# A transformer trunk layer on one core: the mix-out as seven block products, and five held steps in the down projection

## The chip, the core and the metric

The kernel runs on one core of a Trainium2 chip. The metric is device time in microseconds for one launch, the median of several runs. The core has a matrix engine (PE), two engines for elementwise work (VectorE, DVE in the profile, and ScalarE, ACT), GpSimd (POOL) and SyncE (SP). In this kernel SP and POOL issue nearly all transfers between the chip's memory (HBM) and the on-chip tiles. PE writes its sums into eight PSUM banks of 128 x 512 float32.

## What is computed

One layer with 512 tokens of width 1024, all in float32. Cut to the steps that matter here:

```python
def trunk_layer(x, mem):
    h = rms_norm(x, g[0])
    # four branches of width 256, each projected to 1024 and gated
    branch = jnp.einsum('bskc,kcd->bskd', y_stack, w_branch)
    gates = jax.nn.sigmoid((h @ w_gate).reshape(b, s, 4, 1024) + b_gate)
    merged = jnp.sum(gates * branch, axis=2)
    y = merged @ w_mix_out                        # mix-out, 1024 x 1024
    x = x + rms_norm(y, g[1])
    h = rms_norm(x, g[2]); mem_n = rms_norm(mem, g[4])
    y = cross_attention(h, mem_n, wq, wkv, wo)
    x = x + rms_norm(y, g[3])
    h = rms_norm(x, g[5])
    up = causal_dwconv(h @ w_up, conv_w, conv_b)
    gg, val = jnp.split(up, 2, axis=-1)
    y = (jax.nn.gelu(gg) * val) @ w_down          # down projection, 2816 x 1024
    return x + rms_norm(y, g[6])
```

## The kernel before

**Matmuls.** Every large product is made of float32 operands split in two (`split`, L153; for weights `load_unit`, L69): a rounded high part in the format that PE takes, copied by ScalarE (L75), and the rest, subtracted by VectorE (L76). `mm3` (L127) then issues three matmuls, high by high, high by low, low by high.

**Weights.** All weights are read in units of 128 x 1024 (512 KB) in the order of the list `plan` (L81 to L97). `unit()` hands out the next one and keeps `LOOK` = 2 more under way. A unit passes a raw tile (4 buffers) and a split pair (4 buffers each of `whi`, `wlo`). `unit_kept` (L109) splits into general tiles instead, which stay until they are given back.

**Tiles.** Other data lies in 70 general slots of 128 x 512 (`get` and `put`, L54 to L63), handed out first in, first out when the program is written. A slot's new content waits for the last reader of its old one. PSUM has tags A (2 banks), B (4) and C (2).

**Order.** The build fixes the order on each engine. It goes by the order of the code and by when the build reckons that an instruction can start, so an instruction can stand ahead of earlier code that is not yet ready.

**Stages around the change.**
- *Gates* (L657 to L689): for each of the four branches and each of eight column tiles m, a gate product in bank A (24 matmuls) and a branch product in bank C (6), a sigmoid, a product and a sum into `acc[m]`. In the last branch `acc[m]` is split into `merged`.
- *Memory norm* (L692 to L705): four memory tiles, four rows for the statistics (`RowNorm`), the factor spread over a bank C (`bctok`, four small matmuls), eight products on VectorE and four splits.
- *Mix-out* (L747 to L768): x tiles and gains are loaded, then for each column half four token tiles with K = 1024 in eight tiles, four units per half; each bank is squared for the norm and multiplied by the gain.
- *k projection* (L795 to L808): eight units, 24 matmuls of 256 columns each, two banks A. Its time also holds the end of the mix-out's norm, the residual (L771) and the first transposes for the next stage (`turn2`, tile h2T).
- *Down projection* (L1043 to L1161): two halves of tokens, two parities of K tiles and two halves of columns make 2 x 2 blocks. Instead of eight block products it makes seven: p1, p2, p6, p5 in a first pass over the 11 steps of K, and p3, p7, p4 in a second pass, from sums of the operand blocks (`pair_up`, `second_a`, `second_b`) and of the weight blocks. In each pass the last two steps are held back and run product by product, so that a product's sums on VectorE start while PE makes the next one. `down_post` and `finish` do norm, residual and the stores.
- *Weight sums for the down projection* (L637 to L654): `sums_load(i)` reads four quarters of 256 KB on POOL's queue, `sums(i)` makes four VectorE additions and writes four quarters to `wsum` in HBM. Nine of the eleven stand in the gates, one in three gate units; two stand in the k projection.

Of the kernel before, what the change touches and what calls it, by code (L numbers as in the profile page):

```python
# [16 lines left out]
P = 128  # L17
# [9 lines left out]
LOOK = 2  # L27

# [10 lines left out]
def tile_trunk(ctx: ExitStack, tc: tile.TileContext, a: dict, out: bass.AP):  # L39
# [46 lines left out]
    for nm in ("w_mix", "w_k", "w_v", "w_q"):  # L86
        plan += [(a[nm][m], 1024) for m in range(KT)]
# [8 lines left out]
    for i in range(NP):  # L96
        plan += [(a["w_down"][NP + i][:, S:2 * S], S), (wsum[NP + i], 1024)]  # L97
# [536 lines left out]

    quarters = {}

    def sums_load(i):  # L637
        q = [[get("wq") for _ in R2] for _ in R2]
        for r in R2:
            for c in R2:  # L640
                gpsimd.dma_start(q[r][c], a["w_down"][c * NP + i][:, r * S:(r + 1) * S])
        quarters[i] = q

    def sums(i):
        (b11, b12), (b21, b22) = quarters.pop(i)
# [4 lines left out]
        gpsimd.dma_start(wsum[i][:, 0:S], b11)  # L650
        gpsimd.dma_start(wsum[i][:, S:2 * S], b22)
        gpsimd.dma_start(wsum[NP + i][:, 0:S], b21)
        gpsimd.dma_start(wsum[NP + i][:, S:2 * S], b12)
        put(b11, b12, b21, b22)  # L654


    acc = [None] * KT  # L657
    merged = []
    for ki, kb in enumerate(order):
        for m in range(KT):  # L660
# [46 lines left out]
    LO, HI = slice(0, 256), slice(256, S)  # L707
# [45 lines left out]
    yt = [[None, None] for _ in T4]  # L753
    for c in range(2):
        ps = [bank("B" if c == 0 else "AACC"[t], "mo") for t in T4]
        for kp in range(4):
            tok_unit(ps, merged, T4, kp, unit())
        for t in T4:
            n1.square(ps[t], t, c)
            yt[t][c] = get("yt")  # L760
            vector.tensor_tensor(yt[t][c], ps[t], g1[c], op=ALU.mult)
            if t == 0:
                scalar.activation(warm, n1.ss[:, c * 4:c * 4 + 1], AF.Sqrt, scale=0.0, bias=epsc)
    for t in merged:
        put(*t)
# [238 lines left out]
    def pair_up(i):  # L1004
        g0, g1 = g[2 * i], g[2 * i + 1]
        hi, lo = get("gh", F32R), get("gl", F32R)
        for j, t in enumerate((g0, g1)):
            c = slice(j * 256, (j + 1) * 256)
            scalar.copy(hi[:, c], t[:, LO])
            vector.tensor_tensor(lo[:, c], t[:, LO], hi[:, c].bitcast(F32), op=ALU.subtract)  # L1010
        vector.tensor_sub(g1[:, LO], g0[:, LO], g1[:, LO])
        vector.tensor_sub(g0[:, LO], g0[:, LO], g0[:, HI])
        vector.tensor_sub(g0[:, HI], g1[:, HI], g0[:, HI])
        vector.tensor_add(g1[:, LO], g1[:, LO], g0[:, HI])
        gp1[i] = (hi, lo)
# [30 lines left out]
    def down_post(t, c):  # L1046
        n5.square(yt[t][c], t, c)
        if c == (1 if t < 2 else 0):
            n5.add(t, t + 1)
        vector.tensor_tensor(yt[t][c], yt[t][c], g6[c], op=ALU.mult)  # L1050

    def finish(t):
        n5.root(t, t + 1)
        for c in range(2):
            vector.scalar_tensor_tensor(yt[t][c], yt[t][c], n5.col(t), xt[t][c], op0=ALU.mult, op1=ALU.add)
            sync.dma_start(out[t][:, HALF[c]], yt[t][c])
        put(*yt[t])


# [181 lines left out]
```

## Time and profile before

| What | Value |
|---|---|
| Median of 3 runs | 942.09 us (941.8 to 942.45) |
| Profiled execution | 941.86 us, its span 940.0 us |
| Mean granted PE clock | 0.995 of full speed |
| HBM read, written | 119.25 MB, 13.63 MB |
| Matmuls and transposes on PE | 4534 |
| Weight sums in the trace | 11, from 117.7 to 399.3 us |

Times in the profile count from the start of the span. A row of a group gives line, engine, operation, output and inputs, shape and count, then its busy time and the mean of one, then the engine's idle time before it and what ended it. A row of a timeline gives start, length, engine and the same, with the idle time before it in brackets. `PE` is matmuls and `PEld` weight loads beside them. The chain that ended last is the path followed back from the last instruction.

### The profile page before, as it was taken

What the parts mean: (1) busy time and instruction counts of PE and PEld (TensorE: products, weight loads), DVE (VectorE), ACT (ScalarE), POOL (GpSimd) and SP (SyncE); (2) the same over time, 40 slices, a digit from 0 to 9 for tenths busy, and PEclk for the clock granted to TensorE, in tenths of its full rate; (3) what the DMA queues carried; (4) which work ended last, traced back from release to release, by engine and by line L of the source; (5) the groups of instructions that cost most, each with busy time, mean ns of one, the idle gap of its engine ahead of it and who ended that gap; (6) DMA issues with size and microseconds to landing.
All of it is one profiled execution on the core that took longest, in us unless ns stands there. A gap on an engine that the chain in (4) does not pass through costs nothing.

```text
span 940.0 us, 12070 instructions
## 1 busy us (share of the span) xinstructions
PE 922.4 (98%) x4534; PEld 776.9 (83%) x4534; DVE 606.7 (65%) x940; ACT 441.1 (47%) x707; POOL 56.0 (6%) x117
## 2 busy tenths in 40 slices
PE   8999999999999999999999999999999999999994
PEld 7888888888888888889888888988888888888883
DVE  5877569645665566757544845486666666697847
ACT  7836336422342233456433737453443443465642
POOL 1100022401110000300000000000000000000000
PEclk9999999999999999999999999999999999999997
DMA  9432255835564524745522330133322322355552
GB/s 333 141 130 101 101 190 178 290 133 181 192 227 136 195 94 155 241 140 179 180 90 77 125 112 1 48 110 95 107 90 98 104 90 93 120 178 181 166 191 90
DMA packets 43563, 133.67 MB, mean 142 GB/s; under 512 B 6240, under 2 KB 7152, under 8 KB 43504
## 3 DMA queue, kind: packets, MB, share of 16 engines
q1 hardware_dynamic: 36288, 109.81, 35.5%
q0 software_dynamic: 7072, 23.09, 7.1%
q8 instruction: 35, 0.57, 0.2%
q14 instruction: 24, 0.20, 0.1%
q10 hardware_dynamic: 144, 0.00, 0.0%
HBM read 119.25 MB, written 13.63 MB: 141 GB/s over the span
## 4 chain that ended last, share of the span: by engine, by line
PE 94%; DVE 3%; ACT 2%; DMA 0%; issue 0%; SPq 0%; DVEq 0%; ACTq 0%
PE up L130 8%; PE up L128 8%; PE up L129 8%; PE gate L128 6%; PE gate L129 6%; PE gate L130 6%; PE win L128 4%; PE win L129 3%; PE win L130 3%; PE dn L129 3%; PE dn L128 3%; PE dn L130 3%; PE br L128 2%; PE mo L128 2%; PE q L128 2%; PE q L130 2%
## 5 line engine op out<-in xcount | busy, mean ns | idle before, releaser
L76 DVE TENSOR_TENSOR wlo<-raw,whi 128x1024 fp32r<-128x1024 f32 (+1 forms) x181 | 214.3, 1189 | 155.5 <-ACT whi L75 155.0
L75 ACT CAST whi<-raw 128x1024 fp32r<-128x1024 f32 (+1 forms) x181 | 185.1, 1026 | 276.0 <-issue 78.9
L128 PE MATMUL up<-h3h,whi 128*128 128x512 f32 (+1 forms) x368 | 138.2, 375 | 0.0
L129 PE MATMUL up<-h3l,whi 128*128 128x512 f32 (+1 forms) x368 | 138.1, 375 | 0.0
L130 PE MATMUL up<-h3h,wlo 128*128 128x512 f32 (+1 forms) x368 | 138.1, 375 | 0.0
L128 PE MATMUL gate<-xgh,whi 128*128 128x512 f32 x256 | 99.9, 390 | 0.0
L130 PE MATMUL gate<-xgh,wlo 128*128 128x512 f32 x256 | 99.7, 389 | 0.0
L129 PE MATMUL gate<-xgl,whi 128*128 128x512 f32 x256 | 99.6, 389 | 0.0
L129 PEld LDWEIGHTS up<-h3l,whi 128*128 128x128 f32 x368 | 69.3, 188 | 12.6
L128 PEld LDWEIGHTS up<-h3h,whi 128*128 128x128 f32 x368 | 69.3, 188 | 12.5
L130 PEld LDWEIGHTS up<-h3h,wlo 128*128 128x128 f32 x368 | 69.3, 188 | 12.3
L550 DVE SCALAR_TENSOR_TENSOR c<-up,par,c 128x511 f32<-128x511 f32 (+1 forms) x88 | 65.1, 745 | 1.3
L128 PE MATMUL win<-xgh,whi 128*128 128x512 f32 x144 | 57.2, 397 | 0.0
L128 PEld LDWEIGHTS gate<-xgh,whi 128*128 128x128 f32 x256 | 48.1, 188 | 10.0
L130 PEld LDWEIGHTS gate<-xgh,wlo 128*128 128x128 f32 x256 | 48.1, 188 | 10.0
L130 PE MATMUL win<-xgh,wlo 128*128 128x512 f32 x144 | 56.3, 391 | 0.0
L129 PEld LDWEIGHTS gate<-xgl,whi 128*128 128x128 f32 x256 | 48.1, 188 | 9.8
L129 PE MATMUL win<-xgl,whi 128*128 128x512 f32 x144 | 56.1, 390 | 0.0
L356 DVE TENSOR_TENSOR sg<-gate,rb0s 128x512 f32<-128x512 f32 x32 | 22.0, 688 | 44.5 <-PE gate L130 44.3
L128 PE MATMUL dn<-whi,sh 128*128 128x512 f32 x110 | 42.8, 389 | 0.0
L129 PE MATMUL dn<-wlo,sh 128*128 128x512 f32 x110 | 42.8, 389 | 0.0
L130 PE MATMUL dn<-whi,sl 128*128 128x512 f32 x110 | 42.8, 389 | 0.0
(376 smaller groups left out, 1736.3 us busy)
## 6 DMA issues: line engine op xcount, KB each, us to landing
raw<-in_w_up SPq DMA_DIRECT2D x44, 512.0 KB, 3.4
raw<-in_w_gate SPq DMA_DIRECT2D x32, 512.0 KB, 4.1
wq<-in_w_down POOLq DMA_DIRECT2D x44, 256.0 KB, 3.9
wsum<-wq POOLq DMA_DIRECT2D x44, 256.0 KB, 3.3
raw<-wsum SPq DMA_DIRECT2D x22, 512.0 KB, 3.6
raw<-in_w_in SPq DMA_DIRECT2D x18, 512.0 KB, 3.9
raw<-in_w_down SPq DMA_DIRECT2D x11, 512.0 KB, 4.3
raw<-in_w_br SPq DMA_DIRECT2D x8, 512.0 KB, 3.5
```

Source lines behind the costliest of these rows:

```text
L75: scalar.copy(hi[:, :n], raw[:, :n])
L76: vector.tensor_tensor(lo[:, :n], raw[:, :n], hi[:, :n].bitcast(F32), op=ALU.subtract)
L128: tensor.matmul(ps, lhsT=w[0], rhs=x[0], start=first, stop=False)
L129: tensor.matmul(ps, lhsT=w[0], rhs=x[1], start=False, stop=False)
L130: tensor.matmul(ps, lhsT=w[1], rhs=x[0], start=False, stop=last)
L356: vector.tensor_tensor(t, ps, rb0s, op=ALU.mult)
L550: vector.scalar_tensor_tensor(dst[:, s:S], src[:, 0:S - s], pc(wname, (taps - 1 - s) * stride + off), dst[:, s:S], op0=ALU.mult, op1=ALU.add)
```

## The change

The mix-out is computed as the down projection was: token halves, K parities and column halves form 2 x 2 blocks, four steps of two K tiles, seven products in two passes. The bodies of the down projection move into functions that both stages call: `pair_first`, `pair_a`, `pair_b` make the operand sums, `seven` runs the two passes. In `seven` the last `ha` steps of the first pass and the last `hb` of the second are held: the mix-out has 2 and 2, the down projection 2 and 5 (`HOLD`; it was 2 and 2).

The weight sums of the mix-out (four, into `msum`) go first in the queue of weight sums. The queue is now worked by `sums_step`, in every second gate unit from the sixth, with one set loaded further ahead, and in the k projection's units. The operand sums of the mix-out are made pair by pair in the last branch's gates.

For the last five steps of the down projection's second pass the weights are no longer in `plan` but split with `unit_kept` into general slots, made one step ahead.

```diff
+HOLD = 5
@@ plan
-    for nm in ("w_mix", "w_k", "w_v", "w_q"):
+    msum = dp.tile([8, P, 1024], F32, name="msum")
+    for i in range(4):
+        plan += [(a["w_mix"][i], 1024), (msum[i], 1024)]
+    for i in range(4):
+        plan += [(a["w_mix"][4 + i][:, S:2 * S], S), (msum[4 + i], 1024)]
+    for nm in ("w_k", "w_v", "w_q"):
...
-    for i in range(NP):
+    for i in range(NP - HOLD):
         plan += [(a["w_down"][NP + i][:, S:2 * S], S), (wsum[NP + i], 1024)]
@@ operand sums, moved
+    def pair_b(g0, g1):
+        ah, al, b = get("sh", F32R), get("sl", F32R), get("sb", F32R)
+        scalar.copy(ah, g1)
+        vector.tensor_sub(al, g1, ah.bitcast(F32))
+        scalar.copy(b[:, LO], g0[:, LO])
+        vector.tensor_sub(b[:, HI], g0[:, LO], b[:, LO].bitcast(F32))
+        put(g0, g1)
+        return ah, al, b
@@ the two passes
+    def seven(n, first, opa, opb, wua, wub, ha, hb, ready):
+        bks = [[bank(tag, "sv") for _ in T2] for tag in "BBCA"]
+        held, free_later = [], []
+        for i in range(n):
+            wa, ws = wua(i)
+            a, e = first[i], opa(i)
+            f, l = i == 0, i == n - 1
+            todo = [(bks[0], a, 0, wa(0, S), f, l), (bks[1], a, 256, wa(S, 2 * S), f, l),
+                    (bks[2], e, 256, ws(S, 2 * S), f, l), (bks[3], e, 0, ws(0, S), f, l)]
+            if i < n - ha:
+                for p in todo:
+                    product(*p)
+                put(*a, *e)
+            else:
+                held.append(todo)
+                free_later += [*a, *e]
...
+                elif k == 2:
+                    vector.tensor_sub(d0[t], bks[2][t], yt[t][0])
+                    vector.tensor_add(yt[t][0], yt[t][0], bks[1][t])
+                    ready(t, 0, False)
+                elif k == 3:
+                    vector.tensor_sub(d1[t], d0[t], bks[3][t])
...
+        for k in range(3):
+            for t in T2:
+                for todo in held:
+                    product(*todo[k], ts=(t,))
+                if k == 0:
+                    yt[t][1] = get("yt")
+                    vector.tensor_sub(yt[t][1], d1[t], bks[0][t])
+                    ready(t, 1, True)
+                elif k == 1:
+                    yt[t + 2][1] = d1[t]
+                    vector.tensor_sub(d1[t], d1[t], bks[1][t])
+                    vector.scalar_tensor_tensor(d0[t], d0[t], -1.0, bks[1][t], op0=ALU.mult, op1=ALU.add)
+                    ready(t + 2, 1, False)
+                else:
+                    yt[t + 2][0] = d0[t]
+                    vector.tensor_add(d0[t], d0[t], bks[2][t])
+                    ready(t + 2, 0, True)
@@ weight sums
+    sumq = [(a["w_mix"], i, 4, msum) for i in range(4)] + [(a["w_down"], i, NP, wsum) for i in range(NP)]
+    summing = []
+
+    def sums_step(load=True):
+        if len(summing) > 1 or (summing and not sumq):
+            sums(summing.pop(0))
+        if load and sumq:
+            summing.append(sumq.pop(0))
+            sums_load(summing[-1])
@@ gates
-            step = ki * KT + m - 5
-            if step >= 0 and step % 3 == 0:
-                sums_load(step // 3)
-            if step >= 2 and step % 3 == 2:
-                sums(step // 3)
+            if ki * KT + m >= 5 and (ki * KT + m - 5) % 2 == 0:
+                sums_step()
...
-                if ki == 3:
-                    merged.append(split(acc[m], "mg", True))
+                if ki == 3 and m % 2 == 1:
+                    pair = acc[m - 1], acc[m]
+                    mix_first.append(pair_first(*pair))
+                    mix_a.append(pair_a(*pair))
+                    mix_b.append(pair_b(*pair))
@@ mix-out
-    for c in range(2):
-        ps = [bank("B" if c == 0 else "AACC"[t], "mo") for t in T4]
-        for kp in range(4):
-            tok_unit(ps, merged, T4, kp, unit())
...
+    def mix_ready(t, c, last):
+        n1.square(yt[t][c], t, c)
+        vector.tensor_tensor(yt[t][c], yt[t][c], g1[c], op=ALU.mult)
...
+    seven(4, mix_first, mix_a.__getitem__, mix_b.__getitem__, lambda i: (unit(), unit()), lambda i: (unit(), unit()),
+          2, 2, mix_ready)
@@ k projection
-        if m in (2, 4):
-            sums(8 + m // 2)
-        if m in (0, 2):
-            sums_load(9 + m // 2)
+        sums_step()
@@ down projection
+    def w_second(i):
+        if i < NP - HOLD:
+            return unit(), unit()
+        b, ts = unit_kept(a["w_down"][NP + i][:, S:2 * S], S)
+        z, tz = unit_kept(wsum[NP + i])
+        kept_down[i] = ts + tz
+        return b, z
+
+    kept_at = ahead(lambda j: w_second(NP - HOLD + j), HOLD, 1)
...
+    seven(NP, gp1, ahead(lambda i: pair_a(g[2 * i], g[2 * i + 1]), NP, 1),
+          ahead(lambda i: pair_b(g[2 * i], g[2 * i + 1]), NP, 1),
+          lambda i: (unit(), unit()), w_later, 2, HOLD, down_ready)
```

`pair_first` is the body of `pair_up` (L1007 to L1014), `pair_a` that of `second_a`; `down_ready` holds what `down_post` and `finish` did, in the same order for one tile.

More of the change, by code (lines that the diff above doesn't have):

```diff
@@ L1044, in tile_trunk, with down_ready @@
     n5 = TokNorm("n5")
-    def down_post(t, c):
+    def down_ready(t, c, last):
         n5.square(yt[t][c], t, c)
-        if c == (1 if t < 2 else 0):
+        if last:
             n5.add(t, t + 1)
         vector.tensor_tensor(yt[t][c], yt[t][c], g6[c], op=ALU.mult)
[L1052 to L1057, printed above, removed]
@@ new lines, in down_ready, with ahead, at @@
+        if t == 0 and not last:
+            scalar.activation(warm, n5.ss[:, 0:1], AF.Sqrt, scale=0.0, bias=epsc)
+        if last:
+            n5.root(t, t + 1)
+            for h in range(2):
+                vector.scalar_tensor_tensor(yt[t][h], yt[t][h], n5.col(t), xt[t][h], op0=ALU.mult, op1=ALU.add)
+                sync.dma_start(out[t][:, HALF[h]], yt[t][h])
+            put(*yt[t])
+    def ahead(make, n, by):
+        made = []
+        def at(i):
+            while len(made) < min(n, i + 1 + by):
+                made.append(make(len(made)))
+            return made[i]
+        return at
```

207 lines of the change are left out of this document (79 added, 128 removed).

## The prediction

> **What bounds the kernel now.** I read the page first, then the busy time by stretches, then the timelines of the two stages that the change touches.
>
> ```profile
> PE 922.4 (98%) x4534; PEld 776.9 (83%) x4534; DVE 606.7 (65%) x940; ACT 441.1 (47%) x707; POOL 56.0 (6%) x117
> PE 94%; DVE 3%; ACT 2%; DMA 0%; issue 0%; SPq 0%; DVEq 0%; ACTq 0%
> 320.00:371.00 51.00, 51.00 (x228) 42.24 (x227) 29.46 (x38) 18.52 (x24) 0.00 (x0) 1.00 0.43 141
> 371.00:393.00 22.00, 22.00 (x101) 18.27 (x100) 17.05 (x27) 10.50 (x18) 5.47 (x11) 1.00 0.65 214
> 393.00:414.50 21.50, 21.50 (x97) 17.80 (x96) 9.97 (x13) 7.15 (x13) 3.21 (x6) 1.00 0.57 193
> 414.50:441.50 27.00, 26.89 (x221) 26.16 (x220) 23.11 (x37) 19.67 (x42) 0.00 (x0) 1.00 0.43 141
> 928.00:940.00 12.00, 0.00 (x0) 0.00 (x0) 8.19 (x17) 2.65 (x8) 0.00 (x0) 0.60 0.36 132
> ```
>
> In the rows of stretches the columns are length, then PE, PEld, DVE, ACT and POOL busy, granted clock, DMA share, GB/s. PE is the path nearly everywhere: it fills the last gates (320 to 371), the mix-out (371 to 414.5) and nearly all of the k projection behind it. So a matmul taken out is time taken out, as long as PE stays fed. After 928 PE has nothing left, and 12 us belong to DVE, ACT and the stores.
>
> **The mix-out: what is removed.** Before, 2 halves x 8 K tiles x 4 token tiles x 3 matmuls = 192; after, 7 products x 4 steps x 2 token tiles x 3 = 168.
>
> ```profile
> L128 PE MATMUL mo<-whi,mgh x64: 389/389/478, 371.2 to 414.2; 128*128 128x512 f32 x64
> ```
>
> The recorded 389 ns is no price, because matmuls overlap. 63 intervals of three matmuls lie between 371.2 and 414.2: 43.0 / 189 = 0.2275 us each. 24 fewer are **-5.4 us**, if nothing else ends last. The stage would last 168 x 0.2275 = 38.2 us.
>
> **What it adds on VectorE.** These are the stage's groups before, and prices for operations that the trace has elsewhere:
>
> ```profile
> L76 DVE TENSOR_TENSOR wlo<-raw,whi 128x1024 fp32r<-128x1024 f32 x9 | 11.0, 1221 | 11.1 <-ACT whi L75 11.1
> L76 DVE TENSOR_TENSOR wlo<-raw,whi 128x512 fp32r<-128x512 f32 x11 | 7.5, 683 | 0.0
> L1123 DVE TENSOR_TENSOR sl<-c,sh 128x256 fp32r<-128x256 f32 x11 | 4.4, 418 | 0.3 <-PE dn L129 0.3
> L1112 DVE TENSOR_TENSOR d<-d,dn 128x512 f32<-128x512 f32 x2 | 1.4, 678 | 0.0
> L701 DVE SCALAR_TENSOR_TENSOR mem<-mem,par,bctok 128x256 f32<-128x256 f32 x8 | 3.5, 472 | 0.0
> 379.01 1.28 DVE L156 TENSOR_TENSOR meml<-mem,memh 128x512 fp32r<-128x512 f32 x2
> 399.31 0.69 DVE L649 TENSOR_TENSOR wq<-wq,wq 128x512 f32<-128x512 f32 x1
> ```
>
> DVE is busy 17.05 + 9.97 = 27.0 us in 43.5. The change adds: sixteen weight loads for eight, of which four are half wide, so 4 x 1.22 + 4 x 0.68 = 7.6; the last pair's ten half-wide operations and one full, 4.9, for a split of 0.7, so 4.2; and fourteen sums and differences of the products, 14 x 0.68 = 9.5. That is 48.3 us with the two weight sums that lie here now (2 x 4 x 0.69 = 5.5) and 42.8 without them, against 38.2 of PE. The operations of a row overlap by some 0.08 of 0.68 (two of 128x512 take 1.28 at 379.01, not 1.36), so about 0.88 of it, **37.7 to 42.5 us**, is DVE time. The cover that was there (16.5 us idle) is used up, and the stage is limited by two engines at once.
>
> How much of that PE feels is what no row shows. Below: 0, if the weight sums run in the gates and the memory work (eight operations of 0.47 and four of 0.68, 6.5 us) fits between. Above: 48.3 - 38.2 = 10.1, if nothing overlaps. Nearest is the first half of the down projection, which has the same loop and the same loads:
>
> ```profile
> 822.00:873.00 51.00, 51.00 (x226) 42.24 (x225) 41.56 (x69) 32.15 (x53) 0.00 (x0) 1.00 0.59 181
> ```
>
> There DVE is 81% busy and PE loses nothing. The mix-out would stand at 99% or over, so I take **+3.5**.
>
> **What moves around it.** In the gates the longest wait of a weight sum for its quarter was this:
>
> ```profile
> 190.95 0.69 DVE L646 TENSOR_TENSOR wq<-wq,wq 128x512 f32<-128x512 f32 x1 [6.47 <-DMA wq<-in_w_down]
> ```
>
> Each of three pairs adds 10 x 0.42 + 0.68 - 2 x 0.69 = 3.5 us to DVE, and twelve weight sums are done instead of nine (3 x 2.8 us over 250 us); the stretch 320 to 371 has 21.5 us idle, so I cost it at 0 (if a queued sum blocked DVE where the cover is gone, at most those 6.5 us). The new slots matter more. At the end of the gates before, 16 of 70 slots are held; after, 28 operand tiles and 8 quarters, and the free list is first in, first out. Counted along it, the eight x tiles and two gains get slots of xg, and the last memory row gets the one of the last pair's sum.
>
> ```profile
> 275.03 4.12 SPq L750 DMA_DIRECT2D xt<-in_x_rows  x2
> 366.38 1.71 SPq L750 DMA_DIRECT2D xt<-in_x_rows  x2
> 262.08 0.16 DVE L216 TENSOR_TENSOR rsm_parts<-rsm_parts 128x2 f32<-128x2 f32 x1 [1.92 <-ACT row L211]
> row<-in_mem_rows SPq DMA_DIRECT2D x4, 256.0 KB, 4.3
> 380.00:391.00 11.00, 11.00 (x50) 9.13 (x49) 7.16 (x9) 3.87 (x5) 3.79 (x7) 1.00 0.85 288
> ```
>
> So the x loads (8 x 0.25 MB, spread before from 275 to 368) bunch behind the last gate on SP's queue, with the late units of the mix-out behind them, and the memory statistics, done at 262 before, move into the stage. The weights are some eight units ahead (four raw, four split), which is over 20 us at 2.7 us a unit, so I cost the transfers at 0. All bytes asked for from 365 to 409 are 4.5 MB of x, gains and memory, 6 of weights and 2 to 6 of sums: 12.5 to 16.5 MB, which at the 288 GB/s of the last row take 43 to 57 us for 44; the upper end is part of the second rival. The Trainium skill (DMA: Bandwidth & Descriptors, Issuing engines are not separate DMA queues) says that transfers begun on SP and on POOL share the same sixteen engines. By it moving the sums to POOL's queue buys no bandwidth, which the row does not contradict.
>
> Behind the mix-out the k projection lives on DVE too:
>
> ```profile
> 418.06 5.39 DVE L771 SCALAR_TENSOR_TENSOR xt<-yt,rs_n,xt 128x512 f32<-128x512 f32 x8
> 420.61 3.33 PE L786 MATMUL h2T<-ident,xt 128*128 128x128 f32 x24
> ```
>
> Two k tiles fill bank A until 420.6, and the transposes start at the moment when their x tiles are there; the chain has no slack. After, the last product leaves an addition ahead of its square, and the second half's last two products put 3 DVE operations (1.8 us) on each 1.36 us of PE: about 1 us later. Up to one weight sum more falls here (2.8). Between 0 and 4, I take **+1**.
>
> **The down projection's end.** The counts stay: PE ends when it ended before. What changes is the spacing.
>
> ```profile
> 926.95 0.39 PE L130 MATMUL dn<-whi,sl 128*128 128x512 f32 x1
> 931.94 0.63 ACT L724 ACTIVATE sq<-d 128x512 f32<-128x512 f32 x1 [0.48 <-DVE d L1159]
> 932.48 0.19 ACT L724 ACTIVATION_READ_ACCUMULATOR sq<-d 128x1 f32 x1
> 931.83 0.15 DVE L728 TENSOR_TENSOR rs_n<-ss_n 128x1 f32<-128x1 f32 x1
> 932.57 0.61 ACT L732 ACTIVATE rs_n<-rs_n,epsc 128x1 f32<-128x1 f32 x2
> 933.57 2.74 DVE L1055 SCALAR_TENSOR_TENSOR d<-d,rs_n,xt 128x512 f32<-128x512 f32 x4
> 934.35 2.32 SPq L1056 DMA_DIRECT2D out_y<-d  x4
> out_y<-yt SPq DMA_DIRECT2D x4, 256.0 KB, 2.0
> out_y<-d SPq DMA_DIRECT2D x4, 256.0 KB, 2.5
> ```
>
> With two held steps a product of one token tile takes 2 x 3 x 0.2275 = 1.36 us, and DVE has 1.8 to 2.6 us of work for each: it works through a backlog from 927.3 to 936.3, 9.0 us behind PE. With five held steps it takes 3.4 us, and the backlog is gone. Then behind the last matmul: addition 0.68, square 0.63 + 0.19, sum of squares 0.15, root 0.3 (two take 0.61), the gain and reciprocal beside and behind it 0.7, two last operations 1.4 (four take 2.74): 3.9 to 4.0. The gain is 9.0 - 4.0 = **-5.0** (none if a backlog remains; 5.5 if the stores, which land 0.5 us later in fours, speed up as well). What is late next is this same chain, and then the store, 3.7 us from 936.3 to 940.0.
>
> The price is weights. The last five steps' pieces, 5 x 0.75 MB, are split into 30 slots and must all be there when the first held product passes: the second half starts 11 x 18 x 0.2275 = 45.0 before PE's end at 927.3, so at 882.3; PE reaches the held product after six steps of 4.08 (the distance of the two DVE rows below), at 906.8, and its fifth step at 909.5.
>
> ```profile
> 903.98 1.83 DVE L76 TENSOR_TENSOR wlo<-raw,whi 128x1024 fp32r<-128x1024 f32 x2 [2.26 <-ACT whi L75]
> 908.06 1.82 DVE L76 TENSOR_TENSOR wlo<-raw,whi 128x1024 fp32r<-128x1024 f32 x2 [2.25 <-ACT whi L75]
> 900.00:928.00 28.00, 27.34 (x121) 22.32 (x119) 16.53 (x25) 10.82 (x18) 0.00 (x0) 1.00 0.38 130
> ```
>
> DVE idles 2.25 of 4.08 us a step here, waiting for a split buffer that PE frees; kept pieces need none, only raw tiles, from about 891. That leaves 18 us for 3.75 MB (208 GB/s, under the 288 above), 9 us of splits on DVE and as much on ACT. I cost it at **0**; above, the 130 GB/s of the stretch 900 to 928 would make the last piece 10 us late.
>
> **The sum**, against the profiled execution's own 941.86 (its span of 940.0 and 1.86 around it): 941.86 - 5.4 + 3.5 + 1 - 5.0 = 935.96. The median of the runs shown is 942.09, 0.23 more: **936.2 us**.
>
> **Rivals.**
> 1. *Everything is covered.* Stalls under 2 us: the scheduler puts weight sums into idle gates (it ran two sums of the k projection at 385 to 400, in the mix-out). Against it: DVE at 99%. 942.1 - 10.4 = 931.7; 931 to 933.5. Chance 0.22.
> 2. *VectorE becomes the mix-out's bound*, with two or three sums and their transfers inside the stage: its gain is eaten and more, 942.1 - 5.0 - 5.4 + 10.1 = 941.8; 938 to 944. For it: a fixed queue in which a sum waits for its quarter blocks the splits behind it. Against: sums have 400 us until they are needed. 0.17.
> 3. *The end gains nothing*, because late kept weights push what the spacing saves: 942.1 - 5.4 + 4.5 = 941.2. 0.05.
> 4. *Slower: PE stands before the mix-out.* PE's order is fixed, and the program writes the four small matmuls of the memory norm (bctok) ahead of the first product; before, they stood exactly there.
>
> ```profile
> L224 PE MATMUL bctok<-ident,rsm x4: 271/274/275, 370.9 to 371.2; 128*128 128x128 f32 x4
> 389.92 1.28 ACT L763 ACT_TABLE_LOAD   x1
> ```
>
> Now they need a row that loads only when the last pair is split (about 378), then 4.3 to land, a square of 0.8, a table (1.28), a root of 0.3 and a reciprocal of 0.2: ready near 385. If they stay in front, PE idles 14 us: 936.2 + 14 - 3.5 (DVE catches up meanwhile) = 946.7. It decides from 12 us of stall on. Against it: orders follow readiness (h2T stands in the code behind the seventh k tile, and ran behind the second). Chance 0.08. The clock row above falls to 0.60 when PE idles; the Trainium skill (TensorE: Matmul & The Clock Gate, Part 1: The HAM clock gate) has half clock after an idle window of about 3.4 us until as long a busy one. By that this rival would cost some 1.7 us more, an estimate from that page; no run here shows PE restarting after such a gap.
>
> **How the numbers follow.** The forecast, stalls of 2 to 6.5 us and the whole gain at the end (933.5 to 938.5), has 0.48. The range takes in rival 1 and most of 2 and 3: 931 to 941; outside lie rival 4, the top of 2 and 3 (0.08) and the least of rival 1 (0.03). 0.2% is 1.9 us, about what a measurement here can tell from no change. Faster, below 940.2: 0.48 + 0.22 + 0.07 of rival 2 + 0.01 of 3 = 0.78. Within: 0.14. Slower: 0.08.
>
> **What would show it.** PE matmuls of the mix-out 168 over 40 to 43 us, with gaps ahead of products whose split is late; DVE over 90% there; bctok inside the stage, not ahead of it; x loads bunched at 365 to 372; sums in the k projection. At the end DVE finished about 4 us after the last matmul, and no gap in PE near 907 to 910. Wrong would be: mix-out gaps over 7 us, gaps at 907, or PE idle near 371.

## The result, and the profile after

The changed kernel takes **964.2 us** (962.5 to 966.19, four runs) beside 942.27 of the kernel before in the same measurement: a ratio of 1.0232, 95% interval 1.0217 to 1.0246. The forecast was 936.2, with 0.08 for slower. The profiled execution took 963.52 us, its span is 961.8.

The page of the changed kernel, busy time and the chain that ended last:

```profile
PE 928.5 (97%) x4510; PEld 775.5 (81%) x4510; DVE 642.4 (67%) x1019; ACT 452.0 (47%) x737; POOL 72.9 (8%) x149
PE 68%; issue 10%; DMA 9%; DVE 8%; ACT 4%; POOL 2%; DVEq 0%; SPq 0%; POOLq 0%; ACTq 0%
```

PE issues the 24 matmuls less, and yet is busy 6 us longer, at a lower granted clock (0.989 for 0.995); its part of the chain fell from 94% to 68%. Busy time by stretches of the changed kernel (gates, mix-out, k projection to up projection, down projection, and what is behind the last matmul; columns as in the prediction):

```profile
148.40:389.00 240.60, 230.27 (x1022) 187.86 (x1020) 158.57 (x240) 79.91 (x108) 51.12 (x95) 0.97 0.58 196
389.00:434.00 45.00, 40.48 (x174) 31.45 (x173) 36.04 (x56) 24.79 (x42) 3.80 (x7) 1.00 0.73 253
434.00:603.90 169.90, 166.43 (x898) 143.66 (x897) 104.08 (x165) 93.05 (x191) 0.54 (x1) 0.99 0.37 119
846.60:954.30 107.70, 105.68 (x463) 86.33 (x462) 83.20 (x136) 61.72 (x108) 0.00 (x0) 1.00 0.51 166
954.30:961.80 7.50, 0.12 (x1) 0.00 (x0) 3.44 (x7) 1.02 (x3) 0.00 (x0) 0.76 0.38 140
```

The borders are the first matmuls of the stages in the groups of instructions. With the same borders for the kernel before:

| Stage, us | before | after | difference | forecast |
|---|---|---|---|---|
| before the gates | 147.3 | 148.4 | +1.1 | 0 |
| gates | 223.9 | 240.6 | **+16.7** | 0 |
| mix-out | 43.7 | 45.0 | +1.3 | -1.9 |
| k projection to up projection | 164.8 | 169.9 | +5.1 | +1 |
| up projection | 242.8 | 242.7 | -0.1 | 0 |
| down projection on PE | 104.8 | 107.7 | +2.9 | 0 |
| behind the last matmul | 12.7 | 7.5 | -5.2 | -5.0 |

The 1.1 us ahead of the gates lie within what the kernels below show there (146.7 to 149.1). The gates hold most of the loss, 77% of the 21.8 us. The same stretch before:

```profile
147.30:371.20 223.90, 223.90 (x1025) 185.59 (x1024) 138.46 (x193) 80.53 (x102) 30.40 (x56) 1.00 0.53 179
```

Before, PE was busy for all of the 223.9 us; now it stands 10.3 us (240.6 - 230.3) and takes 6.4 us more for its work, at a granted clock of 0.97. How this comes about is seen in the timeline of the changed kernel, 289 to 299 us:

```profile
289.74 0.69 DVE L765 TENSOR_TENSOR wq<-wq,wq 128x512 f32<-128x512 f32 x1 [6.87 <-DMA wq<-in_w_down]
...
289.75 0.39 PE L136 MATMUL gate<-xgh,wlo 128*128 128x512 f32 x1
...
291.48 0.68 DVE L800 TENSOR_TENSOR sg<-br,sg 128x512 f32<-128x512 f32 x1
...
292.22 0.50 PE L134 MATMUL br<-yah,whi 128*128 128x512 f32 x1 [2.08 <-DVE sg L800]
...
296.92 0.69 DVE L762 TENSOR_TENSOR wq<-wq,wq 128x512 f32<-128x512 f32 x1 [4.02 <-DMA wq<-in_w_down]
297.52 0.68 DVE L362 TENSOR_TENSOR sg<-gate,rb0s 128x512 f32<-128x512 f32 x1
...
298.25 0.72 ACT L799 ACTIVATE sg<-sg,par 128x512 f32<-128x512 f32 x1 [13.68 <-DVE sg L362]
298.36 0.77 PE L134 MATMUL gate<-xgh,whi 128*128 128x512 f32 x1 [3.57 <-DVE sg L362]
```

VectorE stands 6.87 us at the last addition of one weight set and 4.02 us at the first of the next, because their quarters haven't landed. The gate operations that empty the PSUM banks (L362, L800) are queued behind. ScalarE's sigmoid gets nothing for 13.7 us. PE has two banks A to fill ahead, at most 2 x 24 x 0.2275 = 10.9 us of gate products. When VectorE stops, at 282.9, it has just read one of them and the other is all but full, so PE has less: it runs on until 290.1, 7.3 us. Then it stands 2.1 us for a bank C (L800) and, after the branch product, 3.6 us for a bank A (L362).

These two stands are 5.7 of the 10.3 us. The next, 2.9 us, is at 172:

```profile
170.25 0.69 DVE L763 TENSOR_TENSOR wq<-wq,wq 128x512 f32<-128x512 f32 x1 [1.18 <-DMA wq<-in_w_mix]
170.86 0.20 DVE L511 RECIPROCAL rsg<-rsg 128x8 f32<-128x8 f32 x1
...
172.15 1.13 PE L519 MATMUL rbg<-ident,rw 128*128 128x128 f32 x8 [2.91 <-DVE rw L513]
```

Here a reciprocal for the norm of one branch stands behind an addition that waits only 1.18 us, and behind four more additions between 165.8, when ScalarE has its input ready, and 168.5. So the work of the additions delays the queue as well as their waits. The other 1.7 us are waits for splits of gate weights.

### The profile page after: what moved, and what is told of

The parts are those of the page before. It is cut to its first block, busy times and chain, and to the rows that moved or that the text cites. A ratio compares the mean times of both kernels' runs of the same rounds, so it can differ in the third digit from the quotient of the medians.

```text
span 961.8 us, 12214 instructions
## 1 busy us (share of the span) xinstructions
PE 928.5 (97%) x4510; PEld 775.5 (81%) x4510; DVE 642.4 (67%) x1019; ACT 452.0 (47%) x737; POOL 72.9 (8%) x149
## 4 chain that ended last, share of the span: by engine, by line
PE 68%; issue 10%; DMA 9%; DVE 8%; ACT 4%; POOL 2%; DVEq 0%; SPq 0%; POOLq 0%; ACTq 0%
PE up L134 8%; PE up L136 8%; PE up L135 8%; PE sv L134 3%; PE sv L135 3%; PE sv L136 3%; PE gate L134 3%; PE gate L135 3%; PE gate L136 2%; PE win L134 2%; PE win L135 2%; PE win L136 2%; DVE wlo L77 2%; DMA wq<-in_w_down 2%; DMA wq<-in_w_mix 2%
## 5 line engine op out<-in xcount | busy, mean ns | idle before, releaser
L362 DVE TENSOR_TENSOR sg<-gate,rb0s 128x512 f32<-128x512 f32 x32 | 22.0, 688 | 33.3 <-PE gate L136 33.2
L799 ACT ACTIVATE sg<-sg,par 128x512 f32<-128x512 f32 x32 | 23.1, 722 | 41.3 <-DVE sg L362 41.2
L134 PE MATMUL sv<-whi,sh 128*128 128x512 f32 x100 | 38.5, 393 | 2.0 <-DVE mem L827 2.0
L135 PE MATMUL sv<-wlo,sh 128*128 128x512 f32 x100 | 39.1, 393 | 1.1 <-DVE wlo L77 1.1
```

What stands on the lines that cost most here:

```text
L134: tensor.matmul(ps, lhsT=w[0], rhs=x[0], start=first, stop=False)
L135: tensor.matmul(ps, lhsT=w[0], rhs=x[1], start=False, stop=False)
L362: vector.tensor_tensor(t, ps, rb0s, op=ALU.mult)
L799: scalar.activation(sg, sg, AF.Sigmoid, bias=pc("bgate", kb * KT + m))
```

## The experiments

Theory: additions that wait for their quarters block VectorE's queue, and the new queue of weight sums makes such waits longer or puts them one behind another. Rivals: the transfers themselves crowd out weights; the operand sums or the slots of the new mix-out cost it; and, within the theory, the number (or rate), the depth or the slots of the sets.

### The two halves of the change apart

`queue_only` is the kernel before with the new queue (`sums_step`, fifteen sets) and the old mix-out:

```diff
-            if step >= 0 and step % 3 == 0:
-                sums_load(step // 3)
-            if step >= 2 and step % 3 == 2:
-                sums(step // 3)
+            if ki * KT + m >= 5 and (ki * KT + m - 5) % 2 == 0:
+                sums_step()
```

> The kernel before, with only the queue of the weight sums changed: fifteen sums instead of eleven, one new load every second gate unit and two loads in flight; the mix-out's four sums are made and not used, the mix-out itself and the down projection stay as before. If the sums in the gates are what cost the time, the stretch from the first gate matmul to the mix-out, 223.9 us before and 240.6 after, is 236 to 242 here, and the whole 955 to 962. If the operand pairs or the slots that the new mix-out holds cost it, the gates stay at 223 to 226 and the whole at 942 to 945.

`no_mix_sums` is the changed kernel with the old cadence and without the mix-out's four weight sums; pieces of the mix-out's own weights are read in their place:

```diff
-        plan += [(a["w_mix"][i], 1024), (msum[i], 1024)]
+        plan += [(a["w_mix"][i], 1024), (a["w_mix"][4 + i], 1024)]
...
-    sumq = [(a["w_mix"], i, 4, msum) for i in range(4)] + [(a["w_down"], i, NP, wsum) for i in range(NP)]
+    sumq = [(a["w_down"], i, NP, wsum) for i in range(NP)]
```

> The changed kernel with the mix-out's four weight sums left out (its products read pieces of the mix-out's own weights in place of the sums), and the eleven sums of the down projection at the cadence of before, one load in three gate units. If the added sums cost the 16.7 us in the gates, that stretch is back at 223 to 226 and the whole is 944 to 950 (964.2 - 16.7 = 947.5, less again if the 4.4 us of the k projection belong to its queued sum). If pairs or slots cost it, the stretch stays above 235 and the whole above 957.

Measured: `queue_only` 960.26 us (ratio 1.0189, 1.0172 to 1.0206), gates 237.1 us; `no_mix_sums` 941.56 (0.9989, 0.9979 to 1.0), gates 224.0. So the queue alone, without any block product in the mix-out, costs 13.2 of the 16.7 us, and without it the rest of the change costs the gates nothing. Operand sums and slots fall as a cause of their own. `no_mix_sums` as a whole is 2.4 us under what was expected for it, and shows that what is left of the change is worth next to nothing, 1 us.

### Depth of the queue

`one_set` is the changed kernel; it loads in one gate unit and adds in the next:

```diff
-            if ki * KT + m >= 5 and (ki * KT + m - 5) % 2 == 0:
-                sums_step()
+            if ki * KT + m >= 5:
+                if summing:
+                    sums(summing.pop(0))
+                elif sumq:
+                    summing.append(sumq.pop(0))
+                    sums_load(summing[-1])
```

> The changed kernel with one set of quarters in flight instead of two: a load in one gate unit, its sum in the next, so as many sums in as many units. If the depth of two (eight quarters held, each sum queued far from its load) costs the gates, the loss of 16.7 us falls under 6 and the whole is 947 to 954. If the rate costs it (one set in two units instead of in three, and its 4 MB of traffic), the loss stays at 14 us or grows, since each sum now waits for quarters that were asked for one unit earlier: 962 to 975.

Measured: 952.68 us (1.0116, 1.0093 to 1.0138). The gates take 234.1 us, of which 2.5 go to the small matmuls of the memory norm (`bctok`) that stand ahead of the mix-out here. So 10.2 of the 16.7 us remain, 7.7 without these: depth is part of it, not all. The whole lies in the range that was expected if depth is the cause, but the gates' loss doesn't (under 6). What remains is a matter of rate or number, which these two runs don't separate.

### The wait on VectorE, or the transfers

Two kernels on top of `queue_only`. `queue_no_adds` drops the four additions of `sums`; `queue_pool_adds` gives them to GpSimd:

```diff
-        vector.tensor_add(b11, b11, b12)
-        vector.tensor_add(b12, b12, b22)
-        vector.tensor_add(b22, b22, b11)
-        vector.tensor_add(b21, b21, b22)
+        gpsimd.tensor_add(b11, b11, b12)
+        gpsimd.tensor_add(b12, b12, b22)
+        gpsimd.tensor_add(b22, b22, b11)
+        gpsimd.tensor_add(b21, b21, b22)
```

> The kernel with the queue alone (960.3), with the four additions of every set left out: quarters are loaded and stored as they came, with the same transfers on the same queue and in the same slots, so the weights that the down projection reads as sums are none. If the loss of 13.2 us in the gates comes of additions that wait on VectorE's fixed queue for their quarters, with the gate chain behind them, it is gone: first gate matmul to mix-out 223.9 to 226, the whole 942 to 947. If it comes of the transfers themselves, which delay weights, rows and the branch inputs, the gates stay over 232 and the whole over 952.

> The kernel with the queue alone (960.3), with the four additions of a set made by GpSimd instead of VectorE: same sets, same slots, same bytes, and nothing on VectorE's queue that waits for a quarter. Unlike the run without additions, a store still waits for its additions, so the loads don't run ahead. If the gates lose because VectorE stands at an addition with the gate chain behind it, they are back at 224 to 227, the k projection at 165 to 166, and the whole is 942 to 946. If the transfers cost it, the gates stay over 231 and the whole over 950. If additions on GpSimd slow VectorE, by whatever they share, the medians of VectorE's groups rise above 0.68 us for 128x512 and the whole is over 950 with PE waiting everywhere in the gates.

Measured: without additions 947.36 us (1.0057, 1.0042 to 1.0072), gates 230.0, between the two expectations: half the loss went, but the loads also ran further ahead, since no store waited for an addition any more (297 GB/s from 180 to 210 us, 261 in `queue_only`). With additions on GpSimd 946.27 (1.004, 1.0026 to 1.0055). Groups and stretches, `queue_only` first:

```profile
L129 PE MATMUL gate<-xgh,whi 128*128 128x512 f32 x256 | 101.0, 394 | 5.9 <-DVE sg L357 5.9
180.00:210.00 30.00, 30.00 (x134) 24.85 (x133) 18.88 (x25) 8.43 (x10) 8.63 (x16) 1.00 0.74 261
270.00:300.00 30.00, 24.11 (x100) 19.52 (x99) 16.72 (x24) 6.77 (x8) 6.94 (x13) 0.89 0.71 228
```

And the same of `queue_pool_adds`:

```profile
L129 PE MATMUL gate<-xgh,whi 128*128 128x512 f32 x256 | 99.9, 390 | 0.0
180.00:210.00 30.00, 30.00 (x134) 24.82 (x134) 14.97 (x16) 10.07 (x12) 22.67 (x29) 1.00 0.78 262
147.80:371.90 224.10, 224.10 (x1024) 185.42 (x1023) 136.50 (x163) 80.78 (x103) 123.78 (x145) 1.00 0.65 218
```

The transfers run as fast (262 GB/s for 261; over the whole gates 218 for 205), a set is in the same slots, an addition takes twice as long on GpSimd, and PE doesn't stand in the gates at all: 224.1 us. This settles it for the queue: having the additions on VectorE's queue costs the 13.2 us, the transfers by themselves don't. The run takes both their waits and their 0.69 us each off VectorE; it doesn't price the two apart. (From the k projection to the up projection it takes 3.2 us longer than before, `queue_only` 4.4; I didn't follow that up.)

### Earlier and later slots

If late quarters do the harm, earlier loads should cure it. `queue_own_slots` (on `queue_only`) takes sixteen slots for quarters alone, which the other tiles then lack until the last sum; `paced` (on the changed kernel) takes those freed last:

```diff
# queue_own_slots
-        q = [[get("wq") for _ in R2] for _ in R2]
+        if not own:
+            own.extend(free.pop(0) for _ in range(16))
+        q = [[own_get() for _ in R2] for _ in R2]
# paced
+        free[:0] = [free.pop() for _ in range(4)][::-1]
         q = [[get("wq") for _ in R2] for _ in R2]
```

> The kernel with the queue alone (960.3), with sixteen slots set aside for the quarters from the first load to the last sum, four sets in rotation, in place of those of the common free list, which hold what matmuls and gate operations were the last to read. Same additions, same transfers. If quarters come late because their loads wait for such a slot, the gates go back to 224 to 229 and the whole to 943 to 950. If they come late because the sixteen engines are full, the gates stay over 233 and the whole over 954. In between, 950 to 954, both share it.

> The changed kernel; only the slots of the quarters are those freed last instead of those freed longest ago, so that a set can't be loaded before the gate unit behind which the program writes it. Same sums, same bytes. If the gates lose because sets are issued far ahead of their place in the code and bunch (28 loads before 180 us against 21 before), the 16.7 us there fall under 6 and the whole is 946 to 954. If they lose because a load waits for a slot that is freed late and its addition then waits on VectorE's queue, later slots make it worse: over 966. If the number of bytes alone counts, 960 to 966.

Measured: 962.49 us (1.0223, 1.0203 to 1.0243) and 979.18 (1.0382, 1.035 to 1.0414), gates 244.1 and 257.9. Both are worse. In `queue_own_slots` all sets are asked for by 230 us, and these are two of its stretches, followed by the row of the gate weights from its issues between 150 and 240 us:

```profile
180.00:210.00 30.00, 29.27 (x134) 24.07 (x133) 21.66 (x32) 8.68 (x11) 16.17 (x32) 1.00 0.98 347
210.00:240.00 30.00, 24.53 (x100) 19.50 (x99) 20.01 (x28) 6.88 (x8) 15.07 (x28) 0.94 0.91 323
raw<-in_w_gate SPq DMA_DIRECT2D x10, 512.0 KB, 6.3
```

The same row of `queue_only`:

```profile
raw<-in_w_gate SPq DMA_DIRECT2D x11, 512.0 KB, 3.8
```

The engines are full (0.98), and a gate unit on SP's queue lands after 6.3 us instead of 3.8. So waiting for a slot had held the loads back, to PE's benefit. The Trainium skill (DMA: Bandwidth & Descriptors, Issuing engines are not separate DMA queues) has transfers begun on either queue interleave on the same 16 engines, and the trace agrees: SP's loads land later (6.3 for 3.8 us) when more of POOL's are under way. In `paced` the opposite happens: the slots freed last are those of the set just stored, and loads and additions wait for that store.

```profile
240.00 0.69 DVE L763 TENSOR_TENSOR wq<-wq,wq 128x512 f32<-128x512 f32 x1 [5.70 <-DMA wsum<-wq]
261.24 1.76 POOL L757 DMA_DIRECT2D wq<-in_w_down  x3 [5.87 <-DMA wsum<-wq]
```

So this kernel didn't test an even pace, as its expectation meant to; it tested a chain of stores and loads, and that is worse.

### Fewer sums in the gates

`sums_in_up` leaves the mix-out's four sums in the gates and writes the other eleven into the steps of the up projection; `nine_six` leaves nine there, six in the up projection, and also takes the slots freed last:

```diff
# sums_in_up
+        if f - 2 < NP:
+            sums_load(later[f - 2])
         cg = up(f)
+        if 0 <= f - 3 < NP:
+            sums(later[f - 3])
         cv = up(NF + f)
# nine_six, beside such an edit
+        free[:0] = [free.pop() for _ in range(4)][::-1]
         q = [[get("wq") for _ in R2] for _ in R2]
```

> The changed kernel with only the mix-out's four sums in the gates, one load in three units as before, and the down projection's eleven sums in the up projection, one in each of its steps. By the run without the mix-out's sums (941.6, of which two sums lie in its mix-out and one in its k projection): the gates 223 to 226, mix-out and k projection 1 to 4 us less than there, so 938 to 941 if the up projection hides 11 x 2.8 us of VectorE and 22 MB more of traffic. If it doesn't, over 945.

> As the run with nine sums in the gates and six in the up projection, but the quarters in the slots freed longest ago and two banks in the k projection, as in the changed kernel. If the number of sets in the gates (nine as before, not fifteen asked for one in two units) decides, and the mix-out's sums are worth no more than any other, the gates are 223.9 to 226 and the small matmuls of the memory norm don't stand in front of the mix-out (7.1 us there): the whole 938 to 943. If the gates lose although they hold nine, because four of them have to be there for the mix-out, over 946.

`sums_in_up`: 946.03 us (1.0036, 1.0023 to 1.0049), gates 223.9. Its mix-out, the k projection's matmuls and its up projection:

```profile
371.30:411.10 39.80, 38.75 (x170) 31.43 (x170) 34.02 (x53) 23.68 (x38) 0.00 (x0) 1.00 0.63 212
411.10:439.30 28.20, 26.11 (x217) 25.64 (x216) 27.81 (x46) 21.89 (x48) 0.00 (x0) 1.00 0.52 169
579.30:828.30 249.00, 243.15 (x1168) 204.60 (x1167) 182.99 (x279) 106.77 (x157) 42.84 (x80) 1.00 0.52 177
```

This is the new mix-out without a weight sum beside it: 39.8 us against 43.7, a gain of 3.9. But from the first k matmul to the up projection it takes 168.2 us against 164.8, and gives 3.4 back: VectorE is busy 27.8 of 28.2 us there. And the sums cost the up projection 6.2 us, so it doesn't hide them.

`nine_six`: 957.6 (1.0169, 1.0150 to 1.0188), and the expectation fell. The gates lose 4.3 us with nine sets, the number before, and PE stands at `bctok` behind the first pass's opening products. Timeline and stretches of 1 us of `nine_six`:

```profile
384.82 1.22 PE L230 MATMUL bctok<-ident,rsm 128*128 128x128 f32 x4 [5.89 <-DVE rsm L204]
382.00:383.00 1.00, 0.00 (x0) 0.00 (x0) 0.86 (x1) 0.98 (x3) 0.00 (x0) 0.52 1.02 236
388.00:389.00 1.00, 1.00 (x4) 0.81 (x3) 1.00 (x4) 0.93 (x2) 0.00 (x0) 0.57 1.01 336
```

This kernel isn't the one that its expectation describes: it still takes the slots freed last, and differs from `nine_six_kb` below in the banks alone. So it doesn't show whether the number of sets decides. `no_mix_sums` has nine sets in the gates at the same cadence, in slots freed longest ago, and its gates take 224.0 us; the 4.3 us can come from the slots, as in `paced`, or from which sets they are. PE's longest stand in these gates, 1.5 us at 362.6, is behind a copy on ScalarE for an operand sum (L670), not behind a weight sum.

Two more on this, `paced_kb` and `nine_six_kb`, with four banks for the k projection and slots freed last; `paced_up_kb` is `sums_in_up` with both:

```diff
-        ps = bank("A", "kT")
+        ps = bank("AABBAABB"[m], "kT")
```

> The kernel with the slots freed last (paced), and the k projection's outputs in four banks (two, two of the mix-out's second half in turn) instead of two. If the k projection loses 4.4 us because its third tile waits for a bank that VectorE, late with the mix-out's last products, hasn't read, the gap in front of the third tile (2.84 us) goes and the whole is 2 to 4 us under paced. If the end of the mix-out's token norm is what counts, PE only waits later, ahead of the transposes: within 1 us of paced.

> Nine sums in the gates (the mix-out's four and five of the down projection's) with the cadence of before, one load in three units, the other six in the up projection, slots freed last, four banks in the k projection. By the stages measured: gates 224 to 226 (nine sums there before), mix-out 39.6 to 41, k projection 1 to 3 less than the 168.2 us from its start to the up projection with the eleven sums there, up projection under 2 us late, the end as with five held steps: 934 to 939. If pace in the up projection is not what cost its 6.2 us, 938 to 943.

> The kernel with the eleven sums in the up projection (946.0), slots freed last and four banks in the k projection. There all eleven sets were loaded from 573 to 692, far ahead of the eleven steps in which the program writes them, and PE stood three times (1.8, 2.0, 2.3 us) with the sums ahead of the gate chain. If that bunching costs, the up projection goes back from 249.0 to 243 to 245 us and the whole is 938 to 942. If the sums cost by their number, it stays over 248 and the whole is over 943.

Measured: 977.44, 957.64 and 953.51 us. The banks are worth nothing: from the k projection to the up projection 167.1 us in `paced_kb` and 167.7 in `paced`, 168.3 in `paced_up_kb` and 168.2 in `sums_in_up`. The wait in front of the third tile (1.7 us in `paced`) is gone in `paced_kb`, but PE waits for VectorE elsewhere, 0.6 us for the split of a weight, 0.6 for a later k tile's bank and 0.5 ahead of the transposes (0.4 in `paced`). VectorE is busy 15.0 of the first 15 us in both, and PE's waits there are all for VectorE; that the norm's end is what counts, as the second expectation has it, is not shown.

`nine_six_kb` missed its range (934 to 943) as `nine_six` did: gates 226.1 us, PE standing 6.9 us at `bctok`, and an up projection of 249.1 with six sums, no shorter than with eleven. In `paced_up_kb` the up projection takes 256.8 us for 249.0, so slots freed last didn't help it. How pace and number share in the 6.2 us stays open.

### Additions on GpSimd in the other kernels

The edit of `queue_pool_adds`, made in the changed kernel, in `sums_in_up` and in `hold_only` (below):

> The changed kernel with all additions of the weight sums made by GpSimd. If VectorE's waits are the cause: gates 224 to 227 (16.7 less), the mix-out without sums on VectorE 39.6 to 41 (as in the run with the sums in the up projection; 45.0 now), k projection 168 (169.9): 964.2 - 15 - 4.5 - 1.7 = 943; 938 to 946. If the transfers are: over 955.

> The kernel with eleven sums in the up projection (946.0), additions by GpSimd. If its 6.2 us there come of VectorE standing at additions, the up projection is back at 242.8 to 244 us and the whole is 939 to 941.5. If not, 945 to 948.

Measured: `pool_adds` 960.18 us (1.0189, 1.0174 to 1.0205), `sums_in_up_pool` 961.29 (1.0199, 1.0184 to 1.0215), both far from what I expected. In `pool_adds` the gates recover 9.9 of 16.7 us (230.7), but one stand of PE is left, by another queue:

```profile
262.49 0.63 ACT L217 ACTIVATE row<-row 128x512 f32<-128x512 f32 x1 [13.38 <-DMA row<-in_mem_rows]
266.64 0.80 PE L134 MATMUL gate<-xgh,whi 128*128 128x512 f32 x1 [4.09 <-ACT whi L76]
```

Now ScalarE stands at a row of the memory norm, with the cast of a gate weight behind it. The mix-out (49.3 us) and the k projection (173.7 to the up projection) got longer, with units of the mix-out and of w_k landing late; why is open. In `sums_in_up_pool` the up projection takes 264.1 us; that VectorE's additions cost it 6.2 is not shown by this.

### The end of the down projection alone

`hold_only` is the kernel before with `HOLD = 5`, nothing else; `hold_only_4` has `HOLD = 4`; `hold_pool` is `hold_only` with additions on GpSimd.

> The kernel before with only the down projection's last five steps taken product by product (before: two), nothing of the mix-out. By the trace after, the end gains 5.0 us (from the last matmul to the end of the span 12.7 before, 7.6 after) and the late kept weights give back 2.8: 942.3 - 2.2 = 940.1; 938.5 to 941.5. If the 2.8 came from the state in which the rest of the change leaves the queues, it is 937 to 938. If the kept weights are worse without it, over 942.

> The kernel with the new end alone (938.1), with four steps held instead of five. A product of one token tile then takes 4 x 3 x 0.2275 = 2.73 us of PE against 1.8 to 2.6 of VectorE, so the tail should stay at 7.3 us behind the last matmul, and 0.75 MB less of kept weights is late: of the 1.9 us by which PE ends later than before, 0.6 to 1.9 should go. 936 to 937.8. If the tail needs the fifth step, 938.5 to 940.

> The kernel with the new end alone (938.1), additions of its eleven sets by GpSimd. VectorE waited 23.6 us for quarters in the gates there and PE lost nothing by it, so nothing is to be had: 937 to 939. If GpSimd's additions slow VectorE, over 940.

Measured: **938.13 us** (0.9952, 0.9938 to 0.9967), 938.57 (0.9963, 0.9948 to 0.9977) and 939.65 (0.9967, 0.9954 to 0.998). `hold_only` beats both kernels, and by a little more than expected, since the kept weights give back 2.2 us and not 2.8. Behind the last matmul it takes 7.3 us (12.7 before), and the down projection on PE 107.0 (104.8). With four held steps PE loses 0.1 us, but the tail is 8.6, so the tail does need the fifth step: the same sum, as far as these runs can tell. `hold_pool` lies between its two expectations and gains nothing.

## Why the prediction was wrong

No rival came near 964.2 us; the slowest gave 946.7.

**Gates: the step that failed.** I costed the new queue "at 0 (if a queued sum blocked DVE where the cover is gone, at most those 6.5 us)". The mechanism in the bracket is the one that happened; that it was priced at nothing, and bounded by one wait, was wrong. I looked for cover in the stretch 320 to 371, where the new operand sums lie, and the loss came between 168 and 304, where quarters are late. I took the longest single wait of before (6.47) for the bound, though PE stands for whatever its lead doesn't cover, again at each wait: at 282.9 the lead was 7.3 us. The wait of 6.87 us, with the addition and a split between it and the read of the bank that PE needed, cost 2.1, and the next, of 4.02, cost 3.6, since PE had no free gate bank left. The slower work behind such stands (6.4 us in the gates) was not in the bound either. The second rival held the sentence that was needed ("a fixed queue in which a sum waits for its quarter blocks the splits behind it"), but for the mix-out alone. The runs put in its place: 13.2 us by the queue (`queue_only`), all of it by the additions on VectorE's queue (`queue_pool_adds`). The other 3.5 in the changed kernel are not taken apart. In `pool_adds`, with no addition on VectorE, ScalarE's wait for a memory row costs the gates; whether it has a part in the changed kernel is not shown.

**Mix-out.** The 168 matmuls kept PE busy for 38.75 us in `sums_in_up`, 38.2 were forecast; in the changed kernel, with the four of `bctok` at 405 inside the stage, as forecast, it is 40.5. The stalls of 3.5 us were too many without sums (1.1) and too few with them (4.5). "Mix-out gaps over 7" did not happen.

**k projection.** Right in mechanism, mis-sized: +1, with 0 to 4 as bounds, against 3.4 with the new mix-out and no sum there (`sums_in_up`) and 5.1 in the changed kernel. It isn't only that additions come later; the third k tile waits 2.7 us for a bank that VectorE has not read, and a later one 0.3:

```profile
L134 PE MATMUL kT<-memh,whi 128*128 128x256 f32 x64 | 19.1, 298 | 3.0 <-DVE kl L924 3.0
```

Weight sums cost there too: `queue_only`, with the old mix-out and a last set added at 433 to 446, loses 4.4 us, and `queue_own_slots`, with all its additions done by 238, 0.1. In `sums_in_up`, of the 5.4 us that the matmuls saved, 3.9 reached the mix-out and 0.5 the k projection's end. A stage of which two engines are the limit gains little by relief for one.

**The end.** Forecast -5.0, measured -5.2, and in the way that was described. Timeline of the changed kernel, its last matmul and the last operations of VectorE:

```profile
954.04 0.39 PE L136 MATMUL sv<-kwh,sl 128*128 128x512 f32 x1
...
954.81 0.68 DVE L744 TENSOR_TENSOR d<-d,sv 128x512 f32<-128x512 f32 x1
...
957.21 1.41 DVE L1164 SCALAR_TENSOR_TENSOR d<-d,rs_n,xt 128x512 f32<-128x512 f32 x2
```

VectorE is done 4.2 us after PE (958.6 and 954.4), 4 were forecast. The kept weights, costed at 0 with a bound of 10, cost 2.9 here and 2.2 alone; "gaps at 907" is where `hold_only` has them (PE stands between 909.1 and 911.7, with the last pieces landing late), and the changed kernel 25 us later:

```profile
932.10 1.66 ACT L123 CAST kwh<-raw 128x512 fp32r<-128x512 f32 x3 [2.06 <-DMA raw<-wsum]
...
936.90 0.50 PE L134 MATMUL sv<-kwh,sh 128*128 128x512 f32 x1 [0.98 <-ACT kwh L123]
```

**The slower rival** had the wrong place: PE did not stand at `bctok` in the changed kernel. It did in `one_set` (2.4 us) and, inside the mix-out, in `nine_six` (5.9) and `nine_six_kb` (6.9). The restart at half clock is seen in `nine_six` too: from 384.8 to about 388.9 us, which costs some 2.0 us. The estimate from the Trainium skill (TensorE: Matmul & The Clock Gate, Part 1: The HAM clock gate) was 1.7.

## What to carry to other kernels

The price of an operation that waits for a transfer on an engine's fixed queue is what stands behind it. Compare each wait, and the work queued around it, with the lead that PE has at that moment (7.3 us at the longest wait here), all along the stage in which the transfers run; waits that follow one another leave no time to rebuild it. Loading earlier is no cure where the transfer engines are near full. Measure the parts of a change apart: here the smallest part, the end of the down projection, was worth 4 us, and the rest cost some 26 (964.2 for 938.1).

## What the runs showed of the hardware

The granted clock fell after shorter stands than I had reckoned with. Stretches of 1 us of the changed kernel, around the stand at 290:

```profile
291.00:292.00 1.00, 0.00 (x0) 0.00 (x0) 1.00 (x2) 0.00 (x0) 0.48 (x2) 1.00 0.18 70
293.00:294.00 1.00, 1.00 (x4) 0.81 (x3) 0.00 (x0) 0.00 (x0) 0.54 (x1) 0.50 0.93 295
302.00:303.00 1.00, 1.00 (x4) 0.81 (x3) 1.00 (x3) 0.00 (x0) 0.78 (x2) 0.54 0.65 250
303.00:304.00 1.00, 1.00 (x6) 0.78 (x6) 1.00 (x2) 0.73 (x1) 0.30 (x1) 1.00 0.72 262
```

PE stood for 2.1 us; the clock halved when it was already working again, and with the second stand stayed so for ten microseconds. In `sums_in_up` a stand of as long left the clock alone:

```profile
675.00:676.00 1.00, 0.00 (x0) 0.00 (x0) 1.00 (x3) 0.00 (x0) 0.34 (x1) 1.00 0.00 0
676.16 0.47 PE L134 MATMUL up<-h3h,whi 128*128 128x512 f32 x1 [2.17 <-DVE c L556]
677.00:678.00 1.00, 1.00 (x6) 0.84 (x5) 0.97 (x3) 1.00 (x2) 0.82 (x2) 1.00 0.52 184
```

So a stand of some 2 us (2.1 there, 2.2 here) may or may not cost a restart. The Trainium skill (TensorE: Matmul & The Clock Gate, Part 1: The HAM clock gate) has the fall after an idle window of about 3.4 us; the runs show it after 2.1, and the measurement decides.

Additions of 128x512 on GpSimd take 1.30 us where VectorE takes 0.69, and VectorE's 128x1024 subtractions rise from 1.222 us on average in `queue_only` to 1.286 in `queue_pool_adds`, its 24 sums of gate products (L691) from 0.688 to 0.852. PE lost nothing by it in the gates. Rows of `queue_pool_adds`:

```profile
L649 POOL TENSOR_TENSOR wq<-wq,wq x15: 1268/1297/2153, 118.0 to 419.8; 128x512 f32<-128x512 f32 x15
L76 DVE TENSOR_TENSOR wlo<-raw,whi 128x1024 fp32r<-128x1024 f32 x170 | 218.3, 1286 | 173.4 <-ACT whi L75 173.1
```
